# Attention scores from pairs of 64-row matmuls, in a trunk layer with three branches

## The chip, the core and the metric

The kernel runs on one core of one Trainium2 chip. The metric is the device time in microseconds (us) of one execution. The engines are named as in the profile: PE is TensorE with its matmuls, PEld are the loads of weights into it, DVE is VectorE, ACT is ScalarE, POOL is GpSimd, SP issues the DMAs.

## What is computed

Two layers of a hybrid trunk work on 1152 tokens (128 of context, 1024 latent), 1024 channels wide. Each layer projects the normalised stream once and feeds three branches: A is windowed attention with 8 heads of 64 channels, each latent block of 128 tokens seeing its neighbours and the cached context; B is a gated linear recurrence; C is differential attention with 4 heads of two softmax maps each, over all tokens. The branches are gated, projected, merged and projected again into the residual. What this case touches are the scores of A and C:

```
def diff_attn(q, k, v, lam, subln, lam_init):
    ...
    def block(qblk):
        s = jnp.einsum('bqhmd,bshmd->bhmqs', qblk, k).astype(jnp.float32) * SCALE
        p = jax.nn.softmax(s, axis=-1)
        pd = p[:, :, 0] - lam * p[:, :, 1]
        return jnp.einsum('bhqs,bshe->bqhe', pd.astype(v.dtype), v)
...
# branch A, one block of 128 queries, its window of keys (the cached context: the same with k_ctx)
s_w = jnp.einsum('bqkgd,bskd->bkgqs', qblk, kblk).astype(jnp.float32) * SCALE
```

All is float32. The dimension summed over in a score is 64, half of the 128 rows of PE.

## The kernel before, in words

Every value that goes into a product is split into a part rounded to fp32r, the format in which the products are taken (hi), and the rest (lo). A projection is then three products: hi by hi, hi by lo, lo by hi (`mm3`, L161 to L163, called for every large product). PE takes its instructions strictly in the program's order; that order is fixed when the program is built, by a planner that follows priorities and its own estimate of times. The attention has the higher priority, and the projections of the next head, the gates and the inputs of the recurrence run between its instructions ("background").

A layer begins with the unit phase (`unit_phase`): the four heads of branch C, one after the other, then branch A in four pairs of heads. For each group of one or two query tiles, `q_conv` transposes the queries (L440), `c_probs` or `a_probs` multiplies them with the keys (L538 and L539, L660 and L661) and computes the softmax, and `c_pv` or `a_pv` transposes the probabilities (L567, L700) and multiplies them with the values. In the profiled execution these phases lie at about 100 to 900 us (first layer) and 1500 to 2300 us (second). Behind each comes the tail with merge, branch products and recurrence, and then the output projection. The modulation stands at the very start: `mod_rows` multiplies with weights of 2 columns (L281) and transposes rows that have 2 partitions (L288).

For a score the 64 channels of hi and of lo of a key block are stacked to 128 rows, and the queries are copied into both halves of the rows before they are transposed (`qdup`), once as hi and once as lo. So a score is two matmuls over 128 rows, and these hold all four products:

```
T.matmul(out=p, lhsT=qh, rhs=kk, start=True, stop=False)
T.matmul(out=p, lhsT=ql, rhs=kk, start=False, stop=True)
```

PSUM has 8 banks of 512 float32 columns. Before, four are a ring for scores and projections (`ps("s")`), three for transposes (`"t"`), one for the sums with values (`"o"`).

Of the kernel before, what the change touches and what calls it, by code (L numbers as in the profile page):

```python
# [14 lines left out]
ALU = mybir.AluOpType  # L15
# [9 lines left out]
# priority offsets: attention of the units, branch products, modulation (beside the tail, w_out; its sums), recurrence  # L25
# [32 lines left out]
# rows of the per-layer table of short vectors  # L58
# [4 lines left out]
def hybrid_dit_kernel(ctx, tc, I, O):  # L63
# [5 lines left out]
    # buffers of each kind in PSUM  # L69
    PSB = {"s": 4, "t": 3, "o": 1}  # L70
# [51 lines left out]
    def rsqrt(x, n, scale, eps=None):  # L122
        """1/sqrt(x*scale + eps) of a [128, n] AP, n <= 12"""
# [15 lines left out]
    def split(hi, lo, raw, eh="A", el="P"):  # L139
        """hi = raw rounded to fp32r, lo = raw - hi"""  # L140
# [6 lines left out]
    def ws_load(wcols, kt):  # L147
        """[kt*128, 128] weight columns -> hi, lo [128, kt, 128]"""
# [29 lines left out]
    def ws_gemm(L, wcols, consume):  # L178
        """[128 cols, tokens] = W^T h^T, per chunk of 384 tokens"""
# [5 lines left out]
    def layer_vectors(l):  # L185
        """generator: loads the rows, two per step, then turns them into columns"""
# [25 lines left out]
    def layer_scalars(D):  # L212
# [12 lines left out]
        # lamc[3] = -(e1 - e2 + lam_init)  # L225
# [11 lines left out]
        # 4*softplus(-lam) = 4*(max(-lam, 0) + log1p(exp(-|lam|)))  # L237
# [21 lines left out]
    def silu_c():  # L259
        """[128, k, s]: silu of the two conditions, latent and context, in columns"""  # L260
# [13 lines left out]
    def mod_rows(D, b0, n):  # L274
        """blocks b0 to b0 + n by TensorE: the conditions' rows, then turned into columns; a step per load"""
# [156 lines left out]
    def q_conv(src, nb):  # L432
# [6 lines left out]
        for b in range(nb):  # L439
            T.transpose(p[:, b, :], e[:, b, :, :].rearrange("p s d -> p (s d)"), ident)  # L440
# [817 lines left out]
```

## Time and profile before

| | before |
|---|---|
| runs, us | 2894.25, 2898.65, 2900.79 |
| median, us | 2898.65 |
| span of the profiled execution, us | 2896.5 |
| PE busy | 2741.7 us, 95% |
| loads of weights (PEld) busy | 2651.9 us, 92% |
| DVE busy | 1753.5 us, 61% |
| ACT busy | 1272.5 us, 44% |
| POOL busy | 908.3 us, 31% |

The span runs from the first to the last instruction of the execution that was profiled; a run's time is taken around the whole execution. The share of PE counts a matmul from its start to the end of its way through the array, and the next one starts before that end; so the shares say which engine is in use, and the starts of following instructions say what one costs.

### The profile page before, as it was taken

How to read it: one execution, taken by the hardware profiler on the slowest of the kernel's cores; microseconds unless marked ns; L12 is line 12 of the kernel's file. 1: busy time of each engine (PE TensorE's matmuls, PEld its weight loads, DVE VectorE, ACT ScalarE, POOL GpSimd, SP SyncE). 2: the span in 40 equal slices, each digit the busy share in tenths (PEclk: the TensorE clock that was granted, in tenths of full speed). 3: DMA queues.
4: the chain of work that ended last, by engine and by line, in shares of the span. 5: the costliest groups of instructions: out<-in, count | busy, mean ns of one | idle time of the engine just before them, and what ended most of it. 6: DMA issues, size and time to landing. Idle time of an engine off the chain costs nothing.

```text
span 2896.5 us, 44162 instructions
## 1 busy us (share of the span) xinstructions
PE 2741.7 (95%) x16745; PEld 2651.9 (92%) x16745; DVE 1753.5 (61%) x4388; ACT 1272.5 (44%) x2569; POOL 908.3 (31%) x700
## 2 busy tenths in 40 slices
PE   8999999999997989998999999999999989899999
PEld 4989999999997989998999899998999979899989
DVE  5797878776536455116967887787665455311162
ACT  4464555566654531212144645555666446212110
POOL 1243344531234342213103343445212333322230
PEclk9999999999999999999999999999999999999999
DMA  6011011012221133114630110110112222311122
GB/s 227 25 33 32 21 32 42 31 52 73 67 75 62 58 128 108 49 41 140 191 107 25 33 34 19 33 48 31 55 63 80 66 66 64 110 41 52 48 89 85
DMA packets 231697, 190.74 MB, mean 66 GB/s; under 512 B 21746, under 2 KB 217660, under 8 KB 231484
## 3 DMA queue, kind: packets, MB, share of 16 engines
q1 hardware_dynamic: 231484, 187.92, 20.5%
q8 instruction: 132, 2.16, 0.3%
q14 instruction: 81, 0.66, 0.1%
HBM read 153.52 MB, written 34.35 MB: 65 GB/s over the span
## 4 chain that ended last, share of the span: by engine, by line
PE 47%; DVE 9%; ACT 3%; issue 2%; DMA 2%; POOL 1%; SPq 0%; DVEq 0%; POOLq 0%; ACTq 0%
PE ps_s L161 13%; PE ps_s L162 13%; PE ps_s L163 13%; DVE macc L110 2%; PE ps_o L709 1%; DVE lr L110 1%; PE ps_t L700 1%; DMA modw<-in_mod_w_dram 1%; DVE P L540 1%; PE ps_t L567 1%; PE ps_s L538 1%; PE ps_s L539 1%; DVE lu L110 1%; POOL li L101 0%; PE ps_s L660 0%
## 5 line engine op out<-in xcount | busy, mean ns | idle before, releaser
L161 PE MATMUL ps_s<-h,wsh 128*128 128x384 f32 x1920 | 661.1, 344 | 52.4 <-DVE yr L110 46.3
L163 PE MATMUL ps_s<-h,wsl 128*128 128x384 f32 x1920 | 655.3, 342 | 0.9 <-POOL wsl L101 0.9
L162 PE MATMUL ps_s<-h,wsh 128*128 128x384 f32 x1920 | 655.2, 341 | 0.0
L161 PEld LDWEIGHTS ps_s<-h,wsh 128*128 128x128 f32 x1920 | 364.7, 190 | 59.1 <-DVE yr L110 48.3
L163 PEld LDWEIGHTS ps_s<-h,wsl 128*128 128x128 f32 x1920 | 363.8, 190 | 2.0 <-POOL wsl L101 1.6
L162 PEld LDWEIGHTS ps_s<-h,wsh 128*128 128x128 f32 x1920 | 364.5, 190 | 0.6
L101 POOL TENSOR_TENSOR wsl<-wsraw,wsh 128x1024 fp32r<-128x1024 f32 x80 | 198.6, 2482 | 386.9 <-ACT wsh L98 184.1
L161 PE MATMUL ps_s<-uwh,h 128*128 128x384 f32 x864 | 297.6, 347 | 4.7 <-ACT h L98 2.1
L162 PE MATMUL ps_s<-uwl,h 128*128 128x384 f32 x864 | 294.9, 343 | 0.1
L163 PE MATMUL ps_s<-uwh,h 128*128 128x384 f32 x864 | 292.9, 345 | 0.0
L110 DVE SCALAR_TENSOR_TENSOR ps_s<-mg,ps_s 128x384 f32<-128x384 f32 x96 | 52.9, 559 | 353.2 <-PE ps_s L163 353.2
L101 POOL TENSOR_TENSOR qkraw<-qkraw,tab 128x384 f32<-128x384 f32 (+2 forms) x92 | 132.0, 1446 | 342.7 <-DVE qkraw L101 228.6
L540 DVE TENSOR_SCALAR_CACHE_REDUCE P<-ps_s 128x384 f32<-128x384 f32 (+1 forms) x400 | 205.5, 539 | 41.0 <-PE ps_s L539 40.0
L101 DVE TENSOR_TENSOR PT<-ps_t,PT 128x512 fp32r<-128x512 f32 (+2 forms) x304 | 187.6, 625 | 59.2 <-ACT PT L98 57.4
L161 PE MATMUL ps_s<-oh,wb 128*128 128x384 f32 x576 | 194.1, 347 | 26.3 <-DVE yr L101 9.4
L98 ACT ACTIVATE PT<-ps_t 128x512 fp32r<-128x512 f32 (+2 forms) x304 | 159.7, 546 | 124.3 <-PE ps_o L163 66.5
L550 ACT ACTIVATE P<-P,csm 128x1152 f32<-128x1152 f32 (+1 forms) x144 | 165.8, 1155 | 97.9 <-DVE csm L105 97.9
L957 ACT ACTIVATE mg<-ps_s 128x384 f32<-128x384 f32 x144 | 69.8, 486 | 307.2 <-PE ps_s L163 176.6
L162 PE MATMUL ps_s<-ol,wb 128*128 128x384 f32 x576 | 194.5, 344 | 0.0
L163 PE MATMUL ps_s<-oh,wb 128*128 128x384 f32 x576 | 194.3, 344 | 0.0
L161 PE MATMUL ps_s<-woh,yh 128*128 128x256 f32 x576 | 166.5, 290 | 11.8 <-DVE xt L101 6.5
L161 PEld LDWEIGHTS ps_s<-uwh,h 128*128 128x128 f32 x864 | 165.0, 191 | 8.5 <-DVE P L540 3.0
(252 smaller groups left out, 6320.8 us busy)
## 6 DMA issues: line engine op xcount, KB each, us to landing
wsraw<-in_w_in_dram SPq DMA_DIRECT2D x80, 512.0 KB, 3.7
wuraw<-in_w_in_dram SPq DMA_DIRECT2D x72, 192.0 KB, 3.5
ol<-osp SPq DMA_DIRECT2D x24, 576.0 KB, 3.8
modw<-in_mod_w_dram SPq DMA_DIRECT2D x16, 512.0 KB, 6.0
woraw<-in_w_out_dram SPq DMA_DIRECT2D x16, 512.0 KB, 4.4
modw<-in_mod_w_dram SPq DMA_DIRECT2D x14, 576.0 KB, 5.5
modw<-in_mod_w_dram SPq DMA_DIRECT2D x19, 384.0 KB, 4.1
wuraw<-in_w_in_dram SPq DMA_DIRECT2D x36, 128.0 KB, 2.3
```

What stands on the lines that cost most here:

```text
L98: A.activation(out=out, in_=in_, func=AF.Copy, scale=scale)
L101: e.tensor_tensor(out=out, in0=a, in1=b, op=op)
L110: V.scalar_tensor_tensor(out=out, in0=a, scalar=s, in1=b, op0=op0, op1=op1)
L161: T.matmul(out=out, lhsT=r(lh), rhs=r(rh), start=first, stop=False)
L162: T.matmul(out=out, lhsT=r(lh), rhs=r(rl), start=False, stop=False)
L163: T.matmul(out=out, lhsT=r(ll), rhs=r(rh), start=False, stop=last)
L538: T.matmul(out=p, lhsT=qh, rhs=kk, start=True, stop=False)
L539: T.matmul(out=p, lhsT=ql, rhs=kk, start=False, stop=True)
L540: V.tensor_scalar(out=S[:, n * c:n * c + n], in0=p, scalar1=1.0, scalar2=NEG, op0=ALU.mult, op1=ALU.max, accum_out=mx[:, mp, c:c + 1])
L550: A.activation(out=Ss[mp][:, 0:n], in_=Ss[mp][:, 0:n], func=AF.Exp, scale=0.125, bias=nm[:, mp:mp + 1], accum_out=acc)
L567: T.transpose(p[:, b, j * 128:(j + 1) * 128], Pm[:, (b0 + b) * 128:(b0 + b + 1) * 128], ident)
L957: A.activation(out=m, in_=p, func=AF.Tanh, scale=0.5)
```

## The change

The halves of the rows now hold two different things, and a score is taken over 64 rows. In branch C these are the two maps of a head, in branch A two heads. `q_conv` transposes a pair as it comes, without copies. `put_k` keeps hi and lo of the keys in buffers of their own. `qk_pair` issues three products for each of the two halves, alternating, and each half writes its own bank of a buffer of two banks. Lo by lo is no longer computed. In branch A the keys of a group are written into both halves, and the last two windows take their keys from two places, each with its own products.

PSUM is laid out anew: two banks for projections and the sums with values, two for transposes, and two buffers of two banks for scores, which branch products and every other output tile also use in the later phases.

```
-    PSB = {"s": 4, "t": 3, "o": 1}
+    PSB = {"s": 2, "t": 2, "q": 2}
...
-    def q_conv(src, nb):
-        e = al("E", "qdup", nb, 2, 64)
-        V.tensor_copy(e[:, :, 0, :], src)
-        acopy(e[:, :, 1, :], src)
-        q = al("Q", "qhl", 2, nb, 128)
-        p = ps("t", nb, 128)
-        for b in range(nb):
-            T.transpose(p[:, b, :], e[:, b, :, :].rearrange("p s d -> p (s d)"), ident)
+    def q_conv(src, nt):
+        q = al("E", "qhl", 2, nt, 128)
+        p = ps("t", nt, 128)
+        for b in range(nt):
+            T.transpose(p[:, b, :], src[:, b, :, :].rearrange("p s d -> p (s d)"), ident)
         acopy(r(q[:, 0]), p)
         tt(V, r(q[:, 1]), p, q[:, 0], ALU.subtract)
...
+    HALF = (slice(0, 64), slice(64, 128))
+    def qk_pair(pp, q, t, kh, kl):
+        for n, (qi, k) in enumerate(((0, kh), (0, kl), (1, kh))):
+            for hf, out in zip(HALF, pp):
+                T.matmul(out=out, lhsT=r(q[hf, qi, t, :]), rhs=r(k[hf]), start=n == 0, stop=n == 2)
...
     def c_probs(L, u, i, q, t):
-            for c in range(3 if i else 1):
-                n = 384 if i else 128
-                kk = r(u.k[mp][:, 3 * c:3 * c + 3, :] if i else u.xk[mp])
-                p = ps("s", n)
-                T.matmul(out=p, lhsT=qh, rhs=kk, start=True, stop=False)
-                T.matmul(out=p, lhsT=ql, rhs=kk, start=False, stop=True)
+        for c in range(3 if i else 1):
+            n = 384 if i else 128
+            kh, kl = (u.k[0][:, 3 * c:3 * c + 3, :], u.k[1][:, 3 * c:3 * c + 3, :]) if i else u.xk
+            pq = ps("q", 2, 512)
+            pp = [pq[:, mp, 0:n] for mp in range(2)]
+            qk_pair(pp, q, t, kh, kl)
...
-        po = ps("o", w)
+        po = ps("s", w)
```

What the planner makes of it stands in the order of PE's instructions. First a place in the first layer, head 0 of branch C, where scores are threaded into a projection. In a row, the line and the operation are followed by the output, the operands (names as in the program: `ck` keys, `qhl` queries, `uwh` and `uwl` or `wsh` and `wsl` weights, `h` the stream, `P` probabilities, `PT` their transposes, `uv` values) and the size of the output. Before:

```order
L162 MATMUL ps_s<-uwl,h 128x384
L538 MATMUL ps_s<-ck,qhl 128x384
L539 MATMUL ps_s<-ck,qhl 128x384
L538 MATMUL ps_s<-ck,qhl 128x384
L539 MATMUL ps_s<-ck,qhl 128x384
L163 MATMUL ps_s<-uwh,h 128x384
L161 MATMUL ps_s<-uwh,h 128x384
L162 MATMUL ps_s<-uwl,h 128x384
L163 MATMUL ps_s<-uwh,h 128x384
L161 MATMUL ps_s<-uwh,h 128x384
L538 MATMUL ps_s<-ck,qhl 128x384
```

A little later in the same head, of the changed program (L444 is the matmul in `qk_pair`, L562 the transpose in `c_pv`):

```order
L163 MATMUL ps_s<-h,wsl 128x384
L161 MATMUL ps_s<-h,wsh 128x384
L444 MATMUL ps_q<-ck,qhl 128x384 x6
L162 MATMUL ps_s<-h,wsh 128x384
L163 MATMUL ps_s<-h,wsl 128x384
L161 MATMUL ps_s<-h,wsh 128x384
L444 MATMUL ps_q<-ck,qhl 128x384 x6
L162 MATMUL ps_s<-h,wsh 128x384
L163 MATMUL ps_s<-h,wsl 128x384
L444 MATMUL ps_q<-ck,qhl 128x384 x6
L562 MATMUL ps_t<-ident,P 128x128 x6
```

Two matmuls for one map's chunk of scores have become six for the chunk of both maps, and between such runs stand three or two matmuls of a projection. The second place is where scores meet the products with values, again in head 0 of the first layer. Before:

```order
L161 MATMUL ps_o<-PT,uv 128x256
L538 MATMUL ps_s<-ck,qhl 128x384 x3
L567 MATMUL ps_t<-ident,P 128x128 x4
L162 MATMUL ps_o<-PT,uv 128x256
L163 MATMUL ps_o<-PT,uv 128x256
```

And of the changed program:

```order
L162 MATMUL ps_s<-PT,uv 128x256
L163 MATMUL ps_s<-PT,uv 128x256
L444 MATMUL ps_q<-ck,qhl 128x384 x2
L161 MATMUL ps_s<-PT,uv 128x256
L162 MATMUL ps_s<-PT,uv 128x256
L444 MATMUL ps_q<-ck,qhl 128x384 x4
L163 MATMUL ps_s<-PT,uv 128x256
L444 MATMUL ps_q<-ck,qhl 128x384
L161 MATMUL ps_s<-PT,uv 128x256
L444 MATMUL ps_q<-ck,qhl 128x384
L162 MATMUL ps_s<-PT,uv 128x256
```

The six of a chunk are now cut into shorter runs, down to a single matmul of 64 rows between two of 128. Counted over the whole program, the 1728 matmuls of 64 rows stand in 332 runs: 96 of them are one matmul long, 81 are six long, the longest are 36. Of the runs, 152 are followed by a transpose and 180 by another matmul. Before, 928 score matmuls stood among the others; 288 transposes of queries are now 144, and 100 of keys are 104.

## Rows read from the trace of the kernel before

**Rows 1.** The page's first part: span; busy us (share of span) and instructions.

```profile
span 2896.5 us, 44162 instructions
...
PE 2741.7 (95%) x16745; PEld 2651.9 (92%) x16745; DVE 1753.5 (61%) x4388; ACT 1272.5 (44%) x2569; POOL 908.3 (31%) x700
```

**Rows 2.** Windows of attention: length; busy us of PE, PEld, DVE, ACT, POOL; PEclk; DMA.

```profile
100.00:600.00 500.00, 479.90 (x3009) 461.88 (x3010) 403.34 (x1237) 267.61 (x564) 216.12 (x220) 0.98 0.10 30
600.00:900.00 300.00, 288.75 (x1750) 281.86 (x1749) 168.25 (x393) 170.57 (x372) 76.77 (x48) 0.98 0.21 68
1500.00:2000.00 500.00, 477.50 (x2994) 459.45 (x2994) 407.64 (x1271) 263.00 (x559) 193.85 (x200) 0.98 0.11 33
2000.00:2300.00 300.00, 298.42 (x1848) 290.32 (x1847) 179.54 (x460) 184.97 (x417) 87.30 (x63) 1.00 0.20 65
```

**Rows 3.** PE's waits, 100 to 900 us: first and last of 18 rows.

```profile
PE ps_s L161 <- DVE yr L110: 8.8, 1, 8.8
...
PE ps_s L161 <- DVE P L540: 0.2, 1, 0.2
```

**Rows 4.** Timeline of PE at 137 us: start, length, line, operation.

```profile
137.64 0.34 PE L162 MATMUL ps_s<-uwl,h 128*128 128x384 f32 x1
137.82 0.33 PE L538 MATMUL ps_s<-ck,qhl 128*128 128x384 f32 x1
137.99 0.33 PE L539 MATMUL ps_s<-ck,qhl 128*128 128x384 f32 x1
138.16 0.33 PE L538 MATMUL ps_s<-ck,qhl 128*128 128x384 f32 x1
138.33 0.34 PE L539 MATMUL ps_s<-ck,qhl 128*128 128x384 f32 x1
138.50 0.34 PE L163 MATMUL ps_s<-uwh,h 128*128 128x384 f32 x1
```

**Rows 5.** Timelines of PE at 621, 319, 313 and 227 us; rows of several merged.

```profile
621.44 0.39 PE L661 MATMUL ps_s<-ak,qhl 128*128 128x512 f32 x1
621.67 0.34 PE L161 MATMUL ps_s<-h,wsh 128*128 128x384 f32 x1
...
319.14 0.28 PE L161 MATMUL ps_o<-PT,uv 128*128 128x256 f32 x1
319.26 0.28 PE L162 MATMUL ps_o<-PT,uv 128*128 128x256 f32 x1
...
313.32 1.03 PE L567 MATMUL ps_t<-ident,P 128*128 128x128 f32 x8
...
227.36 1.05 PE L583 MATMUL ps_t<-one,sq 128*128 128x1 f32 x8
```

**Rows 6.** Loads of weights by line and shape: count | busy us, mean ns | idle before.

```profile
L161 PEld LDWEIGHTS ps_s<-h,wsh 128*128 128x128 f32 x1920 | 364.7, 190 | 59.1 <-DVE yr L110 48.3 <-ACT mg L957 4.7 <-DVE asm L666 3.5
...
L567 PEld LDWEIGHTS ps_t<-ident,P 128*128 128x128 f32 x584 | 68.7, 140 | 17.5 <-DVE P L110 9.1 <-DVE PT L101 3.8 <-PE ps_t L440 1.9
...
L281 PEld LDWEIGHTS ps_s<-modw,sc 128*2 128x2 f32 x64 | 5.6, 92 | 30.2 <-issue 27.2 <-DMA modw<-in_mod_w_dram 2.9
...
L288 PEld LDWEIGHTS ps_t<-ident,mrow 2*128 2x128 f32 x16 | 1.3, 136 | 4.5 <-ACT mrow L98 2.8 <-issue 0.9 <-ACT xsq L1142 0.9
```

**Rows 7.** Timelines of ACT at 38 us, of PE and PEld at 42 us.

```profile
37.73 0.59 ACT L98 ACTIVATE mrow<-ps_s 2x512 f32<-2x512 f32 x1 [9.02 <-PE ps_s L281]
...
40.54 2.31 PE L281 MATMUL ps_s<-modw,sc 128*2 128x512 f32 x5
...
41.83 1.02 PE L281 MATMUL ps_s<-modw,sc 128*2 128x512 f32 x2
42.78 0.41 PE L288 MATMUL ps_t<-ident,mrow 2*128 2x2 f32 x4
...
42.78 0.32 PEld L288 LDWEIGHTS ps_t<-ident,mrow 2*128 2x128 f32 x4 [0.86 <-issue]
43.11 0.09 PEld L281 LDWEIGHTS ps_s<-modw,sc 128*2 128x2 f32 x2
```

More of the change, by code (lines that the diff above doesn't have):

```diff
@@ L482, in qkv_gemm, with k_conv @@
             yield
-    def k_conv(u, cache, kdst):
+    def k_conv(u, cache, runs, put):
         kc = al("E", "kc", 128)
         dma(kc, cache)
-        kt = lambda i: u.kr[:, i, :, :].rearrange("p h d -> p (h d)")
-        for c in range(3):
-            p = ps("t", 3, 128)
-            for t in range(3):
-                b = 3 * c + t
-                T.transpose(p[:, t, :], kt(b + 1) if b < 8 else kc, ident)
-            for d0, d1, s, n in kdst(3 * c, 3):
-                put_k(d0, d1, p[:, s:s + n, :])
-        p = ps("t", 128)
-        T.transpose(p, kt(0), ident)
-        u.x = al("cx", "xkv", 4, 128)
-        u.xk = [u.x[:, 0], u.x[:, 1]]
-        put_k(u.xk[0], u.xk[1], p)
+        for n, blocks in enumerate(runs):
+            p = ps("t", len(blocks), 128)
+            for t, b in enumerate(blocks):
+                T.transpose(p[:, t, :], kc if b == 8 else u.kr[:, (b + 1) % 10, :, :].rearrange("p h d -> p (h d)"), ident)
+            put(n, p)
     def v_conv(u, cache, pair=False):
-        u.xv = [u.x[:, 2], u.x[:, 3]]
         u.v = [al("S", "uv", 9, 128) for _ in range(2)]
@@ L519, in c_kconv, with put @@
         u.k = [al("S", "ck", 9, 128) for _ in range(2)]
+        x = al("cx", "xkv", 5, 128)
+        u.xk, u.xv = (x[:, 0], x[:, 1]), (x[:, 2], x[:, 3])
+        def put(n, p):
+            hi, lo = [k[:, 3 * n:3 * n + 3, :] for k in u.k] if n < 3 else [k[:, None, :] for k in u.xk]
+            put_k(hi, lo, p)
         k_conv(u, I["cache_c_k"][0, L.l, :, h, :, :].rearrange("t m d -> t (m d)"),
-               lambda b0, n: [(u.k[0][:, b0:b0 + n, :], u.k[1][:, b0:b0 + n, :], 0, n)])
+               ((0, 1, 2), (3, 4, 5), (6, 7, 8), (9,)), put)
     def c_probs(L, u, i, q, t):
@@ L648, in a_probs @@
         for t, i in enumerate(tiles):
-            nb, m0 = 1, None
-            if i:
-                row, k0, nb, m0 = WIN[i - 1]
+            win, m0 = WIN[i - 1] if i else (None, None)
+            nb = sum(w[2] for w in win) if i else 1
             n = nb * 128
             S2 = al("P", "PA", 2, 512)
-            for j in range(2):
+            pq = ps("q", 2, 512)
+            pp = [pq[:, j, 0:n] for j in range(2)]
+            o = 0
+            for row, k0, m in win or ((0, 0, 1),):
+                kh, kl = [x[:, k0:k0 + m, :] for x in u.k[kv][row]] if i else u.xk[kv]
+                qk_pair([p[:, o:o + 128 * m] for p in pp], q, t, kh, kl)
+                o += 128 * m
+            for j, p in enumerate(pp):
                 b = 2 * t + j
@@ L657, in a_probs @@
                 Ps.append(S)
-                p = ps("s", n)
-                kk = r(u.k[kv][row][:, k0:k0 + nb, :] if i else u.xk[kv])
-                T.matmul(out=p, lhsT=r(q[:, 0, b, :]), rhs=kk, start=True, stop=False)
-                T.matmul(out=p, lhsT=r(q[:, 1, b, :]), rhs=kk, start=False, stop=True)
                 if m0 is None:
@@ L692, in a_pv @@
             else:
-                row, k0, nb, m0 = WIN[i - 1]
-                vs = [u.v[kv][:, b, :] for b in KROW[row][k0:k0 + nb]]
+                vs = [u.v[kv][:, b, :] for row, k0, m in WIN[i - 1][0] for b in KROW[row][k0:k0 + m]]
             for b0 in range(0, len(vs), 2):
@@ L813, in unit_phase @@
                 i, m = tiles[0], len(tiles)
[L814 removed]
+                q = fg(q_conv, (u.qs[g] if g else u.q)[:, i:i + m, :, :], m)
                 Ps = fg(a_probs, L, g, tiles, q)
@@ L1073, in w_out_phase @@
                 dma(x, x_in(l, i)[:, cs])
-                p = ps("s", 256)
+                p = ps("q", 2, 512)[:, 0, 0:256] if i % 2 else ps("s", 256)
                 ii = slice(i * 128, (i + 1) * 128)
```

68 lines of the change are left out of this document (30 added, 38 removed).

## Prediction

> **What bounds the kernel now.** I read the page's first lines first: TensorE (PE) has work in 2741.7 of 2896.5 us, the vector engine (DVE) in 1753.5 [rows 1]. The median of the runs, 2898.65 us, is 2.2 us above this span, so I make the sum against 2896.5 and add 2 us at the end. Then the stages, since the change touches only the attention of the two layers. It lies in four stretches of the view by windows [rows 2]: PE is busy 479.9 of 500, 288.8 of 300, 477.5 of 500 and 298.4 of 300 us there, at a granted clock of 0.98 to 1.00; DVE 403 of 500 and 168 of 300. So PE sets the end of these 1600 us, and the list of waits says how little else does: in the first layer's 800 us, PE's waits for others come to 33 us in 18 rows, from 8.8 us (which already belongs to the stage behind) down to 0.2 [rows 3]. A microsecond added to PE's own queue in attention comes out at the end nearly whole, and a microsecond taken off also.
>
> Busy time is no price, since a matmul's row lasts 0.33 us while the next starts sooner. I take starts from the timeline. Scores and projections follow each other every 0.17 to 0.18 us at 384 columns, and nothing opens between L162 and L538 [rows 4]; I use 0.175. At 512 columns it is 0.23, at 256 0.12. Eight transposes of 128 columns take 1.03 us with the last lasting 0.27, so 0.11 each; eight matmuls of one column, where only the load of 128 columns of weights can matter, take 1.05 with the last lasting 0.25, so 0.11 each too [rows 5]. That is the price of a load when nothing hides it behind a longer stream.
>
> **The scores themselves.** Before: 768 matmuls of 384 columns and 64 more in branch A at 0.175, 192 of 512 at 0.23, 64 of 128 at 0.11: 134 + 11 + 44 + 7 = 197 us. After, by the order of the changed program, 1728 matmuls of 64 rows: 1200 of 384 columns, 240 of 512, 144 of 256, 144 of 128, in pairs, one for each half of the rows. No row of this kernel has two such halves at work at once, so I bound their cost from both sides. From below, both matmuls of a pair, loads and streams, take the time of one: 600 x 0.175 + 120 x 0.23 + 72 x 0.12 + 72 x 0.11 = 149 us. From above, nothing overlaps: twice the streams, 298 us. In between, the two streams run side by side but the loads of weights go in one after another. A load here does not get cheaper with fewer rows: the transposes that load 2 rows (L288) take 136 ns, those of 128 rows 140 [rows 6]. Then the load is the limit, 0.11 us for each of the 1728 matmuls (0.23 for a pair of 512 columns, the same), 190 us. I take this middle value as the likeliest: in all of today's rows the next load goes beside the running stream, and none shows two loads at once. So three products instead of four bring 7 us, not the quarter that counting products would give.
>
> **Transposes.** Queries are no longer copied into both halves, so 144 of the 288 transposes fall away; the keys take 4 more. 140 x 0.11 = 15 us less. The copies on DVE and ScalarE that fed them go too; neither engine is the bound, so this can return only as part of PE's 33 us of waits in each layer.
>
> **Going between whole and half rows.** This is the term that decides. The kernel before has one place where PE turns to weights that use only a part of the array and back: the modulation at the start. L281 loads 2 columns of 128 rows, L288 loads 2 rows. The L281 matmuls start every 0.43 us (the fourth of five at 41.83, the first at 40.54), so the fifth at 42.26, and the next instruction should start at 42.69. It starts at 42.78, 0.09 late, and its load begins only then, with an idle of 0.86 us before it put down to nothing ("issue") [rows 7]; what it waits for, the row that ScalarE copies (mrow), was done at 38.32. On the way back the last of four loads, which take 0.32 us together with 0.136 for the last, began at 42.96, and the next load at 43.11: 0.15 instead of 0.06 later, 0.09 late again [rows 6, 7]. So, as I read it, such a turn empties the pipeline, and the load behind it is no longer hidden. The part of a load that is paid then is the difference between 128 columns and 2: 190 less 92 ns, 0.10 us, or for a transpose 140 less 92, 0.05 [rows 6].
>
> [...]
>
> How often? The program's order answers: the 64-row matmuls stand in 332 runs, as the pieces quoted with the change show, because scores are threaded between the projections and the products with values; 96 of the runs are a single matmul. Each run is entered (0.09 + 0.10) and left, 180 times toward a matmul (0.19) and 152 times toward a transpose (0.09 + 0.05): 63 + 34 + 21 = 119 us. And the last matmul of a run has to stream to its end, 0.175 us where I counted 0.11: 332 x 0.065 = 22 us.
>
> **PSUM.** Four banks for everything and one for the sums with values become two, with the scores' four apart; transposes have two where they had three. What could be late is a projection's chunk while the values' sum holds one of the two banks. The nearest price is PE's present waits, 33 us in a layer's attention [rows 3]: at best they shrink to nothing, at worst they double. With less work on DVE and a slower PE they should shrink; I take 10 us off over both layers. In the last stage the branch products move to the scores' banks, and four banks serve as before: nothing.
>
> **Sum.** -7 - 15 + 119 + 22 - 10 = +109 us; 2896.5 + 109 + 2 gives 3007 us, 3.7% slower.
>
> **The rivals.**
> *Loads side by side.* If two halves load at once as well, a pair costs what one costs: 149 instead of 197 us, and no tail of 22: -48 - 15 + 119 - 10 = +46, 2944 us. For it: the halves share no rows. Against it: nothing in the trace shows two loads at once. [...]
> *No overlap at all.* The halves take turns: 298 instead of 197, -15, +119, -10: +195, 3093 us. For it: every pair of rows today is one stream behind the other. Against it: the two halves have their own rows and their own banks.
> *No price for the turn.* If 64 rows of 128 columns behave as the whole array, nothing is drained and loads stay hidden; then -7 - 15 (and no tail) = -22, 2877 us, or with loads side by side -63, 2836 us. This one ends on the other side. For it: the two observed turns involve 2 columns or 2 rows. Against it: the same 0.09 us at both. It decides from the price of a turn: with 664 turns the change is faster only if one costs under 0.03 us with loads in turn, or under 0.095 with loads side by side.
>
> **How the numbers follow.** Loads in turn with turns paid 0.47; loads side by side, paid, 0.18; no overlap, paid, 0.13; no price 0.20, of which something near 0.12 at 2877; the rest is small. The likeliest case alone spans about 2970 to 3045 us: the price of a turn is known to a hundredth or two (664 x 0.02 = 13 us), and PSUM to 30. The range of 2925 to 3095 us takes in the first two cases whole and most of the third, about 8 in 10. Under 0.2% (6 us) a measurement of this kernel can't tell a difference; the only way there is a turn of nearly the deciding price, 0.03. Faster 0.20, slower 0.77.
>
> **What would show it.** Starts of 64-row matmuls 0.11 us apart within a run (0.09 or less: loads side by side; 0.175: no overlap). Before and behind each run an idle of PE put down to issue, the load beginning late. The transposes of queries counted 144. Attention stretches longer by some 50 us a layer, the stage behind them as long as before. The prediction is wrong if the rows inside runs are dense and the rows around them also: then the turn is free; or if PE in attention starts to wait for ScalarE or DVE by far more than 33 us a layer: then the banks are the cause.

## The result, and the profile after

The changed kernel takes 3142.7 us (median of four runs, 3142.35 to 3150.07) against 2899.4 of the kernel before (2894.25 to 2900.79). The ratio is 1.085, with a 95% interval of 1.084 to 1.087: 243 us more. The prediction had the direction (slower), but its 3007 us were 136 short and its range ended at 3095.

The page's first part answers to [rows 1]:

```profile
span 3140.6 us, 44957 instructions
...
PE 2869.9 (91%) x17245; PEld 2639.2 (84%) x17245; DVE 1736.9 (55%) x4276; ACT 1230.2 (39%) x2457; POOL 896.7 (29%) x700
```

PE was busy 95% of the span and is now 91%: the span grew by 244 us, PE's busy time by 128. The same four windows as in [rows 2]:

```profile
100.00:600.00 500.00, 448.87 (x2753) 389.66 (x2751) 340.97 (x1006) 210.99 (x427) 170.30 (x177) 0.93 0.09 28
600.00:900.00 300.00, 281.34 (x1733) 251.72 (x1732) 177.81 (x508) 161.52 (x385) 83.93 (x72) 0.98 0.16 51
1500.00:2000.00 500.00, 445.83 (x2886) 398.68 (x2885) 346.81 (x1005) 186.93 (x425) 122.00 (x122) 0.94 0.19 59
2000.00:2300.00 300.00, 268.90 (x1657) 238.89 (x1655) 201.19 (x587) 140.12 (x307) 114.67 (x118) 0.94 0.11 33
```

In 500 us of the first layer PE was busy 480 us before, at a granted clock of 0.98; now 449, at 0.93. For the first the prediction's sum had only the -10 us of PSUM, for the second no term. PE's waits (48 to 915 us; total, times, longest), which answer to [rows 3], first six of 26:

```profile
PE ps_t L492 <- DVE ak L101: 11.0, 3, 7.1
PE ps_s L162 <- DVE PT L101: 8.0, 8, 2.2
PE ps_q L444 <- DVE P L535: 7.4, 10, 1.9
PE ps_q L444 <- ACT qhl L98: 6.9, 6, 2.2
PE ps_s L161 <- ACT PT L98: 5.7, 4, 2.0
PE ps_s L161 <- ACT h L98: 4.9, 5, 1.8
```

All 26 rows come to 76 us, those of the second layer to 86; over the same stages they were 25 and 23 before. No row is large: PE waits a little everywhere, for the two engines that empty PSUM, at times for a bank (L444 for DVE's reading of earlier scores), at times for an operand that they make (L162 for PT).

Inside the runs of half rows the timeline of PE shows this, at 166 us (answers to [rows 4]):

```profile
165.91 0.33 PE L161 MATMUL ps_s<-h,wsh 128*128 128x384 f32 x1
166.18 0.79 PE L444 MATMUL ps_q<-ck,qhl 64*128 64x384 f32 x6
166.90 0.44 PE L162 MATMUL ps_s<-h,wsh 128*128 128x384 f32 x1
167.18 0.34 PE L163 MATMUL ps_s<-h,wsl 128*128 128x384 f32 x1
```

Six matmuls of 64 rows take 0.72 us from their first start to the start of the next instruction. Three streams of 0.175 are 0.525, so the two halves run side by side. The loads do as well (PEld at 146 us):

```profile
146.41 0.47 PEld L444 LDWEIGHTS ps_q<-ck,qhl 64*128 64x128 f32 x6 [0.64 <-DVE P L535]
```

Six loads within 0.47 us, and each lasts 0.18 to 0.19: in the trace the two loads of a pair start 3 ns apart (146.412 and 146.415), and so do its two matmuls (146.414 and 146.417). That was the prediction's second case, loads side by side, and not the one it took.

Around the runs the price of the turn is there as worked out. From 165.91 to 166.18 are 0.27 us instead of 0.175; the run takes 0.72 instead of 0.525; the first matmul behind it 0.28 instead of 0.175. That is 0.095 + 0.195 + 0.105 = 0.39 us for a run with two borders, 0.2 each, as the prediction had it (0.09, by its reading of the rows for emptying the pipeline, and 0.10 for a load that is no longer hidden).

**Where the 243 us are.** I sort the distances between the starts of successive matmuls, from the first projection of the first layer to the last matmul of the kernel. After a matmul of 384 columns up to 0.175 us is *stream* (0.232 for 512, 0.118 for 256, 0.11 for a transpose, nothing to the partner of a pair that starts with it). What is more, up to one stream and only where the granted clock was 0.50, is *half clock*. At a change between half and whole rows up to 0.21 us, and behind the first matmul after it up to 0.13, are *border* (0.4 and 0.26 at half clock). Of the remainder, distances over 0.3 us are *waits*, the others *rest*. The caps are choices, so a term is good to some 10 us. The kernel before ran again beside every experiment, at 2894 to 2900 us; ratios and differences of an experiment to it are against those runs. For all kernels of this study (us; the last column is the median of the runs):

| kernel | stream | borders (number) | half clock | waits | rest | median |
|---|---|---|---|---|---|---|
| before | 2560 | 0 | 43 | 156 | 85 | 2899 |
| after | 2515 | 109 (664) | 85 | 278 | 101 | 3143 |
| new_banks | 2565 | 0 | 110 | 361 | 125 | 3215 |
| pairs_old_banks | 2579 | 152 (894) | 55 | 128 | 75 | 3044 |
| whole_rows | 2502 | 0 | 113 | 362 | 94 | 3130 |
| six_whole | 2641 | 0 | 61 | 248 | 94 | 3105 |
| whole_old_banks | 2497 | 0 | 58 | 174 | 85 | 2866 |
| one_half | 2562 | 184 (896) | 73 | 126 | 62 | 3062 |
| new_banks_one_half | 2567 | 218 (1008) | 170 | 279 | 84 | 3370 |
| pob_atomic | 2511 | 141 (478) | 197 | 402 | 110 | 3415 |
| before_t2 | 2559 | 0 | 47 | 234 | 93 | 2995 |
| before_sums_in_s | 2561 | 0 | 66 | 184 | 81 | 2945 |
| before_own_scores | 2559 | 0 | 73 | 265 | 100 | 3047 |
| own_sums | 2560 | 0 | 105 | 312 | 100 | 3136 |
| singles | 2564 | 0 | 107 | 360 | 98 | 3183 |
| after_own_sums | 2518 | 115 (688) | 153 | 430 | 102 | 3357 |
| half_transposes | 2546 | 0 | 63 | 198 | 95 | 2957 |
| half_transposes_pool | 2544 | 0 | 58 | 212 | 90 | 2960 |

After against before: -45 stream, +109 borders, +42 half clock, +122 waits, +16 rest. The two terms that the prediction put at -10 and at nothing, waits and clock, are more than the borders. The added waits lie in the two unit phases: 59 us before and 182 after (48 and 162 by the rows of waits above), with 97 and 96 outside them. This sorts PE's time; it doesn't say what taking one term away would give back. The experiments ask that.

### The profile page after: what moved, and what is told of

Same layout as the page of the kernel before. It is cut to its first block, busy times and chain, and to the rows that moved or that the text cites. A ratio compares the mean times of both kernels' runs of the same rounds, so it can differ in the third digit from the quotient of the medians.

```text
span 3140.6 us, 44957 instructions
## 1 busy us (share of the span) xinstructions
PE 2869.9 (91%) x17245; PEld 2639.2 (84%) x17245; DVE 1736.9 (55%) x4276; ACT 1230.2 (39%) x2457; POOL 896.7 (29%) x700
## 5 line engine op out<-in xcount | busy, mean ns | idle before, releaser
L161 PE MATMUL ps_s<-h,wsh 128*128 128x384 f32 x1920 | 670.6, 350 | 32.7 <-ACT mg L953 23.2
L162 PE MATMUL ps_s<-h,wsh 128*128 128x384 f32 x1920 | 662.2, 345 | 0.0
L161 PEld LDWEIGHTS ps_s<-h,wsh 128*128 128x128 f32 x1920 | 369.2, 192 | 46.7 <-ACT mg L953 25.4
L162 PEld LDWEIGHTS ps_s<-h,wsh 128*128 128x128 f32 x1920 | 369.1, 192 | 3.7 <-issue 3.5
L161 PE MATMUL ps_s<-uwh,h 128*128 128x384 f32 x864 | 309.1, 359 | 18.6 <-ACT h L98 6.9
L162 PE MATMUL ps_s<-uwl,h 128*128 128x384 f32 x864 | 303.3, 351 | 4.5 <-POOL uwl L101 4.3
L163 PE MATMUL ps_s<-uwh,h 128*128 128x384 f32 x864 | 301.2, 352 | 0.0
L110 DVE SCALAR_TENSOR_TENSOR ps_q<-mg,ps_q 128x384 f32<-128x384 f32 x96 | 53.8, 560 | 357.9 <-PE ps_q L163 356.8
L535 DVE TENSOR_SCALAR_CACHE_REDUCE P<-ps_q 128x384 f32<-128x384 f32 (+1 forms) x400 | 199.1, 540 | 72.9 <-PE ps_q L444 72.6
L161 PE MATMUL ps_q<-oh,wb 128*128 128x384 f32 x576 | 196.4, 349 | 24.0 <-DVE yr L101 19.5
L101 POOL TENSOR_TENSOR qkraw<-qkraw,tab 128x384 f32<-128x384 f32 (+2 forms) x92 | 118.6, 1300 | 311.7 <-DVE qkraw L101 218.0
L162 PE MATMUL ps_q<-ol,wb 128*128 128x384 f32 x576 | 201.1, 349 | 4.2 <-POOL ol L101 4.2
L444 PE MATMUL ps_q<-ck,qhl 64*128 64x384 f32 x1152 | 175.8, 383 | 27.8 <-ACT qhl L98 14.6
L163 PE MATMUL ps_q<-oh,wb 128*128 128x384 f32 x576 | 199.8, 348 | 0.0
L101 POOL TENSOR_TENSOR uwl<-wuraw,uwh 128x1152 fp32r<-128x1152 f32 (+1 forms) x36 | 89.0, 2472 | 308.9 <-ACT uwh L98 260.7
```

Source lines behind the costliest of these rows:

```text
L101: e.tensor_tensor(out=out, in0=a, in1=b, op=op)
L110: V.scalar_tensor_tensor(out=out, in0=a, scalar=s, in1=b, op0=op0, op1=op1)
L161: T.matmul(out=out, lhsT=r(lh), rhs=r(rh), start=first, stop=False)
L162: T.matmul(out=out, lhsT=r(lh), rhs=r(rl), start=False, stop=False)
L163: T.matmul(out=out, lhsT=r(ll), rhs=r(rh), start=False, stop=last)
L444: T.matmul(out=out, lhsT=r(q[hf, qi, t, :]), rhs=r(k[hf]), start=n == 0, stop=n == 2)
```

## The experiments

**1. The layout alone: new_banks.** The kernel before with the new banks; both maps of a chunk in one buffer (so the loop over chunks goes around that over maps), scores over whole rows as before.

```
-    PSB = {"s": 4, "t": 3, "o": 1}
+    PSB = {"s": 2, "t": 2, "q": 2}
...
+            pq = ps("q", 2, 512)
...
-                p = ps("s", n)
+                p = pq[:, mp, 0:n]
...
-        po = ps("o", w)
+        po = ps("s", w)
```

> The kernel before with nothing but the changed kernel's layout of PSUM: two banks for projections and sums with values, two for transposes, two buffers of two banks for scores; a score is still two matmuls over 128 rows, and both maps of a chunk fill the two banks of one buffer. No matmul of 64 rows, no turn. Theory 'turns' (runs of 64-row matmuls cost PE about 0.19 us at each border, and nothing else matters): 2890 to 2915 us, PE waits in attention near the 25 us a layer of before. Theory 'banks' (the new layout lets PE wait for the engines that empty PSUM, 76 and 86 us a layer in the changed kernel instead of 25 and 23, and the clock falls behind such waits): 2990 to 3080 us, with PE waits in attention of over 60 us a layer.

3215.2 us, ratio 1.109 (1.107 to 1.111): 317 us, more than the whole change, and beyond what either theory said. Waits +205, half clock +67. The layout costs, without a pair in it. Its waits in the second layer's unit phase, first four of the list:

```profile
PE ps_q L539 <- DVE P L541: 18.2, 24, 2.2
PE ps_s L711 <- ACT PT L98: 11.7, 9, 2.8
PE ps_t L568 <- DVE P L110: 11.7, 13, 1.3
PE ps_s L161 <- ACT PT L98: 8.4, 9, 1.5
```

Outputs in all three rings appear, but only the first row is a wait for a bank, that of scores which DVE has still to read. The others wait for an operand: the transposes for P from DVE, the products with values for PT, as the groups of the same stage show:

```profile
L161 PE MATMUL ps_s<-PT,uv 128*128 128x256 f32 x144 | 44.2, 307 | 8.5 <-ACT PT L98 8.4
L711 PE MATMUL ps_s<-PT,uv 128*128 128x256 f32 x226 | 42.7, 302 | 19.2 <-ACT PT L98 11.7 <-DVE PT L101 6.5 <-DVE gate L110 0.7
```

As I read it, PE's order is planned so that something else stands where a bank or an operand is not yet ready; where the planned cover is too short, the wait shows up at whatever comes next. So the rows tell that PE waits, not which ring is to blame; experiments 6 to 10 ask that.

**2. The pairs alone: pairs_old_banks.** The changed kernel, each half in its own bank of the old ring of four.

```
-    PSB = {"s": 2, "t": 2, "q": 2}
+    PSB = {"s": 4, "t": 3, "o": 1}
...
-            pq = ps("q", 2, 512)
-            pp = [pq[:, mp, 0:n] for mp in range(2)]
+            pp = [ps("s", n) for _ in range(2)]
```

> The changed kernel with the PSUM layout of before (four banks for scores and projections, three for transposes, one for sums with values); each half of a pair has its own of the four banks. The scores stand in 447 runs here instead of 332, so there are 894 borders. Theory 'turns and banks': pairs side by side save 48 us, transposes 15, and 447 runs cost about 447 x 0.19 entering, 249 x 0.19 and 198 x 0.14 leaving = 160 us: about +97, 2980 to 3010 us, with attention's PE waits back at about 30 us a layer. Theory 'pairs alone' (all of the 243 us comes from the half rows, and banks have no part): 0.73 us for each of 332 runs gives at least 3140, and 3200 us or more with 447.

3044.4 us, 1.051 (1.049 to 1.052): 146 us more than before, 98 less than the change with its banks. PE's waits are below those of before (12 and 17 us a layer); the first two rows of the first layer:

```profile
PE ps_t L492 <- DVE ukr L101: 2.6, 1, 2.6
PE ps_s L444 <- DVE P L534: 2.4, 3, 1.8
```

The time is 34 us above the expected range, and the timeline shows where it goes, at 307 us:

```profile
307.08 0.39 PE L161 MATMUL ps_o<-PT,uv 128*128 128x256 f32 x1
307.40 0.79 PE L444 MATMUL ps_s<-ck,qhl 64*128 64x384 f32 x3
308.12 0.39 PE L162 MATMUL ps_o<-PT,uv 128*128 128x256 f32 x1
```

Three matmuls of one half take the 0.79 us that six of both halves took above. Where the second bank came later, the planner issued one half's three products alone; 806 of the 1728 streams have no partner beside them, and the stream term is 2579 instead of 2497 us. With a buffer of two banks this is rarer (112 streams in the changed kernel), but the buffers take banks from the rest of the kernel.

**3. and 4. No borders: whole_rows and whole_old_banks.** In the changed kernel, and in pairs_old_banks, three matmuls over all rows stand for the three pairs; they mix the scores of the two halves.

```
-        for n, (qi, k) in enumerate(((0, kh), (0, kl), (1, kh))):
-            for hf, out in zip(HALF, pp):
-                T.matmul(out=out, lhsT=r(q[hf, qi, t, :]), rhs=r(k[hf]), start=n == 0, stop=n == 2)
+        for out, qi, k, first, last in ((pp[0], 0, kh, True, False), (pp[0], 0, kl, False, True), (pp[1], 1, kh, True, True)):
+            T.matmul(out=out, lhsT=r(q[:, qi, t, :]), rhs=r(k), start=first, stop=last)
```

> The changed kernel with three matmuls over 128 rows in place of the six over 64 (two into the first bank, one into the second), which take PE's stream the same time as three pairs side by side; the scores of the two maps or heads are mixed by this, so that what is computed is not the reference's. Layout of PSUM, copies and transposes stay. No border between half and whole rows is left. Theory 'turns and banks': the 664 borders at 0.18 to 0.2 us go, 119 to 130 us, and the waits stay: 3010 to 3030 us. If the half clock of the changed kernel also came from the borders: 2940 to 2980. Theory that a border costs nothing (banks alone are the cause): 3130 to 3150 us.

> The pairs with the PSUM layout of before (pairs_old_banks, 3044 us), with three matmuls over 128 rows in place of six over 64: the scores of the two maps or heads are mixed, and no border between half and whole rows is left. In the changed layout the same edit gave back 13 us of 243. Theory 'hidden borders' (a border always takes PE about 0.19 us; in the changed layout PE had to wait for emptied banks anyway, so that time without borders became waits): here, where PE does not wait, the 894 borders give back 160 us or more: 2830 to 2880 us, below the kernel before by about the 63 us of side-by-side scores and fewer transposes. Theory 'borders cost little' (13 us is their whole price, and the form of the pairs is what is slow): 3020 to 3045 us.

whole_rows: 3129.8 us, 1.080 (1.078 to 1.081). Without any border the changed kernel is only 13 us faster; the waits are 84 us longer and the half clock costs 28 more. whole_old_banks: 2865.9 us, 0.990 (0.988 to 0.992), 178 us below pairs_old_banks: 152 of borders and 82 of streams without partners, less 46 of waits and 3 of half clock and 10 of rest. It is the only one here under the time of before. Its stream term is 63 us below; as three whole matmuls count like three pairs side by side, the 48 + 15 us that the prediction had for the scores and the transposes come out by construction. What the run shows is what is left of them at the end, 28 us, as the other terms eat more than half. So the idea would be worth about 1% if turns were free, every stream had a partner and banks were not short.

With these runs the two layouts stand beside each other three times, with nearly all else alike: new_banks is 317 us over before, the changed kernel 98 over pairs_old_banks, whole_rows 264 over whole_old_banks. The layout costs time each time. The planner makes a new order for each kernel, so what is shown is the layout together with the order planned for it.

**5. The border alone: one_half.** The kernel before, its PSUM and number of matmuls unchanged; the second product of a score over 64 rows.

```
-                T.matmul(out=p, lhsT=ql, rhs=kk, start=False, stop=True)
+                hf = slice(64 * mp, 64 * mp + 64)
+                T.matmul(out=p, lhsT=ql[hf], rhs=kk[hf], start=False, stop=True)
...
```

> The kernel before, where the second product of each score (lo of the queries by the keys) is taken over only the 64 rows that hold hi of the keys, so that lo by lo is left out; as many matmuls of as many columns as before, the same PSUM. 544 matmuls of 64 rows in 448 runs, 896 borders. Theory 'turns': 0.19 us entering and 0.14 to 0.19 leaving, 150 to 170 us: 3040 to 3070 us, with PE's waits for ScalarE and DVE no longer than before. If only the drain is paid and the load stays hidden, about 0.1 us a border: 2980 to 3000. If a border costs nothing: 2890 to 2910 us.

3062.0 us, 1.056 (1.054 to 1.058): +164 us, inside the range of theory 'turns'. Its timeline has the price bare, whole and half rows in turn:

```profile
143.29 0.44 PE L540 MATMUL ps_s<-ck,qhl 64*128 64x384 f32 x1
143.66 0.44 PE L538 MATMUL ps_s<-ck,qhl 128*128 128x384 f32 x1
144.03 0.44 PE L540 MATMUL ps_s<-ck,qhl 64*128 64x384 f32 x1
144.40 0.33 PE L161 MATMUL ps_o<-PT,xkv 128*128 128x128 f32 x1
```

```profile
143.66 0.19 PEld L538 LDWEIGHTS ps_s<-ck,qhl 128*128 128x128 f32 x1 [0.19 <-issue]
144.03 0.18 PEld L540 LDWEIGHTS ps_s<-ck,qhl 64*128 64x128 f32 x1 [0.19 <-issue]
```

Starts are 0.37 us apart instead of 0.175, and every load starts with its matmul, after an idle that nothing explains ("issue"), instead of beside the stream before. 0.195 us a border; 896 of them at that would be 175, and 184 were counted.

**6. to 10. Which banks.** Five divisions of the eight banks in the kernel before, scores over whole rows throughout (s projections, t transposes, o sums with values, c scores):

```
-    PSB = {"s": 4, "t": 3, "o": 1}
+    PSB = {"s": 5, "t": 2, "o": 1}            # before_t2
+    PSB = {"s": 5, "t": 3}                    # before_sums_in_s: ps("o", ..) -> ps("s", ..)
+    PSB = {"s": 2, "t": 3, "o": 1, "c": 2}    # before_own_scores: scores ps("c", n)
+    PSB = {"s": 2, "t": 2, "o": 1, "c": 3}    # own_sums
+    PSB = {"s": 2, "t": 2, "c": 4}            # singles: sums in s
```

> The kernel before with one of the three banks for transposes given to the ring of scores and projections (five, two and one). Which part of the new layout costs 317 us without any pair? Theory 'transposes' (two banks for transposes are too few, since a bank is held until ScalarE and DVE have copied it): most of it, 3050 us or more. Theory 'projections' (two banks for projections, of which the sums with values take one for long): 2895 to 2930 us here, since projections have more banks than before.

> The kernel before with the new layout, but the four banks of the scores each by itself instead of two buffers of two: two banks for projections and sums, two for transposes, four for scores; the branch products and the output stay with the two of the projections. new_banks, with the pairs of banks, took 3215 us. Theory 'pairs of banks' (a buffer of two is free only when both halves are emptied, so two buffers are too few): near 2900 to 2960 in attention's share, that is a unit phase of 770 to 800 us instead of 900. Theory 'projections': unit phases of 870 to 910 us as in new_banks. The stages behind can be longer than in new_banks by the narrower ring there.

> As singles (two banks for projections and sums, two for transposes, four single ones for scores; 3183 us, unit phases of 892 and 893 us), but one bank of the scores goes to the sums with values: projections two, transposes two, sums one, scores three. Theory 'sums' (a sum holds one of the two banks of the projections through all its blocks of keys, so that a projection can't begin while the one before is copied): the unit phases fall most of the way, to 780 to 830 us each, 2960 to 3060 us in all. Theory 'two banks for projections are too few in any case': 860 to 890 us, and 3120 to 3180 in all. If the scores were what wants banks, longer than in singles.

> The kernel before with its ring of four divided: two banks for projections, two for scores; three for transposes and one for sums as before. Against own_sums one bank more for transposes and one less for scores. Theory 'sums': with sums and transposes as before only the division is left, and that costs little: unit phases 765 to 790 us, 2900 to 2950 us. Theory 'two banks for projections are too few': unit phases of 830 us and more, over 3020 us.

> The kernel before, sums with values in the ring of scores and projections, which gets the bank of the sums: five and three banks. Theory 'sums': what hurts is a sum in a ring of two; in a ring of five four are left for the others, as before: 2890 to 2920 us. If sharing a ring is itself what hurts (the order in which its banks are given out): 2950 us or more.

2995, 3183, 3136, 3047 and 2945 us (ratios 1.034, 1.100, 1.082, 1.051, 1.016, each to within 0.003). No single theory came out. The two unit phases together, 1531 us before, are 1582 in before_t2, 1785 in singles, 1657 in own_sums, 1655 in before_own_scores and 1581 in before_sums_in_s; new_banks has 1804. From these: that buffers of two must be empty together costs little (new_banks over singles, 19, with the loops exchanged as well). A bank taken from the transposes and given to the common ring costs 51. Sums in the common ring, which has five then, cost 50, where I had expected nothing. Taking the scores out of the common ring, so that projections and scores have two banks each, costs 124 with all else as before. And putting the sums into the two of the projections costs 127 more (singles over own_sums, although singles has a bank more for scores). The last two are the greater part of the 273 us from before to new_banks. They stand in a row: 124 for the divided ring, 3 for a bank moved from transposes to scores (own_sums over before_own_scores), 127 for the sums, 19 for the pairs of banks. A third bank for transposes was worth 51 beside a common ring and about nothing here, so such prices don't carry from one division to another. Theory 'sums' was half right: they matter most where they sit in a ring of two.

**11. Longer runs: pob_atomic.** pairs_old_banks with the six matmuls of a chunk as one piece for the planner.

```
+        with tc.tile_critical():
+            for n, (qi, k) in enumerate(((0, kh), (0, kl), (1, kh))):
...
```

> The pairs with the PSUM layout of before, and the six matmuls of a chunk issued in one piece, with nothing between them: 239 runs of half rows instead of 447, the shortest six long. Theory 'price per border': 208 runs less at 0.36 us each, 75 us: 2955 to 2985 us. Theory 'price per half-row matmul' (their number, 1728, stays): 3030 to 3050 us. If the pieces hold banks longer and PE waits for DVE because of it, the gain is smaller, with PE's waits in attention above the 12 to 17 us a layer of pairs_old_banks.

3414.6 us, 1.180 (1.178 to 1.182), against both theories. The order has 239 runs as meant, and only 18 streams without partner. But PE's waits are 167 and 172 us a layer, and two of their rows name, by the profile, what a piece waited for:

```profile
PE ps_s L445 <- DVE csm L539: 11.6, 6, 2.6
PE ps_s L445 <- POOL ol L101: 7.9, 2, 4.0
```

A score reads neither `csm` (the maxima behind it) nor `ol`. The piece waits for more than its operands, and the run says nothing of the price of a border.

**12. Fewer transposes: half_transposes, half_transposes_pool.** The kernel before; a pair of query blocks is transposed as it comes, and both halves are filled behind the transposes, by ScalarE and DVE alone or with the second halves by GpSimd.

```
-        e = al("E", "qdup", nb, 2, 64)
-        V.tensor_copy(e[:, :, 0, :], src)
-        acopy(e[:, :, 1, :], src)
...
+        for b in range(nb // 2):
+            T.transpose(p[:, b, :], src[:, 2 * b:2 * b + 2, :].rearrange("p m d -> p (m d)"), ident)
...
+            for hf in (slice(0, 64), slice(64, 128)):
+                acopy(r(qt[hf, 0, :, mp, :]), p[s])
...
```

> The kernel before with the one part of the change that saves PE time without half rows or new banks: the query tiles are transposed a pair at a time, 144 transposes instead of 288, and the two halves are filled from PSUM by four copies of ScalarE and four subtractions of DVE over 64 rows, instead of two copies ahead of the transposes and two operations behind them. 144 transposes less at 0.11 us: 16 us, 2876 to 2888 us. The other theory: the eight short operations hold the bank of the transposes longer and the scores begin later; PE waits for them, 2895 to 2930 us.

> half_transposes (2957 us), in which a bank of the transposes is emptied by four operations of ScalarE and DVE over 64 rows, into half of the rows each, and the other halves are then filled by four copies of GpSimd. Theory 'DVE is late': the eight operations delay DVE's reading of scores (PE's wait for it is 21 us there), and with four less most of the 16 us of PE time comes through: 2875 to 2890 us. The other theory: the scores wait for GpSimd instead, 2900 to 2960 us.

2957.0 us (1.020, 1.018 to 1.022) and 2960.4 (1.022, 1.020 to 1.024). The 14 and 16 us of stream are saved, as priced, and 42 and 56 us of waits and 20 and 15 of half clock come in their place. With GpSimd the wait for DVE's reading of the scores falls from 21 to 8 us and others take its place. Why a longer way from the queries to the scores costs so much was not settled: other orders are planned in both.

**13. Borders in the new layout: new_banks_one_half, six_whole.** The first puts the edit of one_half into new_banks. The second is the changed kernel with each of the six matmuls over all rows, which mixes the scores of the two halves. Its edit:

```
             for hf, out in zip(HALF, pp):
-                T.matmul(out=out, lhsT=r(q[hf, qi, t, :]), rhs=r(k[hf]), start=n == 0, stop=n == 2)
+                T.matmul(out=out, lhsT=r(q[:, qi, t, :]), rhs=r(k), start=n == 0, stop=n == 2)
```

> new_banks (scores over whole rows in the new layout, 3215 us) with the edit of one_half: the second product of each score over only the 64 rows that hold hi of the keys, lo by lo left out. 544 matmuls of 64 rows and, each alone or nearly, up to 896 borders or more are added. In the layout of before the same edit cost 164 us. Theory 'hidden borders' (in the new layout PE waits for emptied banks anyway, and the time of a border only shortens such a wait): 3215 to 3270 us, with PE's waits in attention well below the 205 us of new_banks. Theory 'a border always adds its price': 3365 to 3390 us, waits as before.

> The changed kernel with all six matmuls of a chunk over 128 rows (the scores are mixed by this): no borders, and no two side by side, in nearly the order of the changed kernel (1719 of 16973 matmuls stand at another place; in whole_rows, with three, nearly all did). By the starts of following matmuls in the traces, the changed kernel's two unit phases have 1316 us of streams, 109 at borders, 182 of waits over 0.3 us and 54 of half clock; six streams instead of three pairs add about 131 us, and no border takes away 109. Theory 'order' (borders and waits stand side by side in the changed kernel; in whole_rows only another order made the waits longer): 22 us more, 3150 to 3175 us, waits of 160 to 190. Theory 'ScalarE and DVE set the time' (PE's time, borders or streams, fits into waits): waits fall by about as much as streams grow, and the time is 3060 to 3120 us, with waits under 120.

new_banks_one_half: 3369.8 us, 1.163 (1.160 to 1.165), 155 us over new_banks. 'Hidden borders' falls by its time, and only in part is anything hidden: of 218 us at borders only 82 disappear from the waits and 41 from the rest, and the half clock takes 60 back. six_whole: 3105.4 us, 1.073 (1.071 to 1.075). Six streams one after the other are 37 us faster than six in pairs: +126 of stream, -109 of borders, -24 half clock, -30 waits, -7 rest. Neither theory's numbers held whole; waits of 150 us in the unit phases lie between. Against whole_rows it has 139 us more stream and is yet 24 us faster, with 114 less waits and 52 less half clock. So here less work for PE did not come out at the end: with less of it PE waited longer. It is no rule of this layout, since in new_banks_one_half most of the added work did come out (155 of 218 us).

**14. Another division for the pairs: after_own_sums.** The changed kernel with one buffer of two banks for the scores, and a bank of their own for the sums.

```
-    PSB = {"s": 2, "t": 2, "q": 2}
+    PSB = {"s": 2, "t": 3, "o": 1, "q": 1}
...
```

> The changed kernel with another division of the eight banks: two for projections, three for transposes, one for the sums with values, and one buffer of two for the scores, in place of two, two and two buffers of two. Theory 'rings of projections and transposes' (scores need few banks; a sum in the ring of the projections and a third bank less for transposes are what costs): unit phases of 820 to 855 us instead of 864 and 876, fewer waits, 3050 to 3110 us. Theory 'scores': a single buffer of two can't be filled while it is emptied: 3150 us or more, with waits of scores for DVE's copies on top of the list.

3357.2 us, 1.160 (1.157 to 1.163), the second theory. First rows of the waits of the whole kernel:

```profile
PE ps_s L161 <- ACT mg L953: 79.7, 79, 5.1
PE ps_q L444 <- DVE P L535: 75.1, 54, 2.7
```

The scores wait for DVE to empty their only buffer (75 us, where the changed kernel has 13), and in the stages behind the projections for the merge wait for ScalarE to read them (80 us, there 23). So for pairs in buffers of two, one buffer is too few. Two are half of PSUM, and other ways to divide the other half than that of the change were not run.

## Why the prediction was wrong, step by step

- *What bounds the kernel* held for the kernel before: there PE's microseconds come out at the end (one_half: +164 for 184 at borders). It was then taken to hold for the kernel after, where 109 us of borders taken away gave back 13 (whole_rows).
- *The scores themselves*: the step "I take this middle value as the likeliest", loads one after another, failed. Pairs run side by side with their loads; -7 should have been near -48, and the tail of 22 does not exist. With the transposes that would be -63; the changed kernel has -45, since 112 streams find no partner (112 x 0.175 = 20). The bound from below was the right value, but for those. (The number of score matmuls before is 1088, as the sums have it; the 928 in the section on the change is a slip.)
- *Transposes*: -15 held as stream. half_transposes, which fills the halves by eight operations behind the transposes where the change has two, came out 57 us longer; what the shorter way costs in the changed kernel can't be told from the rest.
- *Turns*: 119 us predicted, 109 counted at the same 332 runs; the price (0.2 us with the load) came from two rows of a wholly different shape and held. That 64-row matmuls would pay it at both ends of a run was the author's estimate, which no row of before shows; the runs showed 109 us at 664 borders (0.16 each) in the changed kernel and 0.195 us a border in one_half, with loads that begin only with their matmul. That it is the pipeline that empties there is the author's reading and was not shown.
- *PSUM* is the step that failed by most: "at best they shrink to nothing, at worst they double ... I take 10 us off". The waits grew by 122 us, and the granted clock, for which the sum had no term, cost 42 more. PE's waits in a kernel with rings of four and three banks were no bound for rings of two; as I read it, they are what is left over after an order was planned round its banks. new_banks shows the cost of the layout without the pairs, +317, and pairs_old_banks the pairs without it, with waits of 12 and 17 us a layer instead of 76 and 86. Even the worst case named, a doubling, adds 33 us a layer, 66 over both, and the span of the likeliest case took 30. (The sums of the rival without a price for the turn, -22 and -63, leave the -10 out.) The prediction had named the sign, waits by far more than 33 us a layer, "then the banks are the cause"; it had given it no price.
- *Nothing in the last stage*: about right. The two stages behind are 18 and 17 us longer, of which 28 are streams: 154 more matmuls of projections and 12 of attention now come after the first branch product.
- By the prediction's own rival with loads side by side the sum was +46. With all terms as counted, -45 + 109 + 122 + 42 + 16 = +244. So the 136 us that the prediction was short are a difference: 190 too little for waits, clock and rest, 55 too much for scores, tail and turns. That the two partly cancel is luck. And the sign: no price for the turn would not have saved it here, as whole_rows shows (3130).

What stays open: why 109 us of borders taken away give back 13 in whole_rows. That its waits are longer is shown, and its order is another one in part: with the scores left out, 2590 of the other 15517 matmuls of PE stand at another place by operands and size (in six_whole 1101). The expectation of six_whole says nearly all; a count by place in the whole order comes out that way, since three matmuls for six shift the place of all that follow. six_whole keeps more of the order and changes the streams. How much is the order and how much the layout was not separated. A kernel with pairs that beats the one before was not found. whole_old_banks is 28 us below before, and a run costs about 0.39, so by this estimate it would need fewer than about 70 runs of half rows in the old banks, all with partners; there are 447.

## What to carry to other kernels

Bound a change of PSUM by running the layout alone, not by the waits of the present one: here waits of 33 us a layer stood beside 317 us for the layout. A run of half-row matmuls costs PE about 0.39 us at its two ends here, a little more than two streams of 384 columns (0.35), so by this estimate half rows can pay only in few and long runs; no kernel here shows that they do. And where a stage waits for other engines, work taken off PE can return as waits and as a lower granted clock, as in whole_rows (109 us less at borders, 84 more of waits and 28 more of half clock).

## What the runs showed of the chip

The granted clock also fell where no wait stands ahead. Windows of one_half (columns as in [rows 2]); from 141 to 148.2 us PE changes 17 times between whole and half rows:

```profile
141.00:148.20 7.20, 7.20 (x27) 4.04 (x25) 5.69 (x20) 1.79 (x6) 6.61 (x11) 1.00 0.00 0
148.20:151.60 3.40, 3.40 (x10) 3.07 (x11) 1.77 (x10) 2.60 (x5) 1.37 (x2) 0.50 0.01 2
151.60:156.00 4.40, 4.40 (x22) 3.59 (x22) 1.98 (x4) 3.96 (x7) 2.49 (x1) 1.00 0.32 92
```

By its busy share PE was never idle; yet the clock was granted at 0.50 for 3.4 us behind that stretch. The share hides the borders, since a matmul's row there lasts 0.44 us instead of 0.33: sorted as above, 3.8 of the 7.2 us are streams and 3.6 borders. Over the two unit phases one_half has 133 us at half clock where the kernel before has 41, with PE's waits at 26 instead of 48 us. That it is the borders, and not the half rows at work alone or something else, is not shown: pairs_old_banks has 894 borders and 85 us at half clock, whole_old_banks none and 85 too, with waits of 29 and 55 us. Behind a wait it looks like this, in the changed kernel:

```profile
168.50:171.80 3.30, 1.31 (x9) 0.67 (x9) 3.05 (x12) 2.91 (x6) 0.64 (x1) 0.99 0.00 0
171.80:178.60 6.80, 4.88 (x19) 4.04 (x20) 6.80 (x16) 1.20 (x2) 2.37 (x1) 0.50 0.22 61
```

In another such stretch, at 435 us (granted 0.50 from 434.6 to 444.8 us), matmuls that go one after the other cost 0.32 us instead of 0.175:

```profile
435.07 0.52 PE L161 MATMUL ps_s<-h,wsh 128*128 128x384 f32 x1
435.39 0.52 PE L162 MATMUL ps_s<-h,wsh 128*128 128x384 f32 x1
435.71 0.52 PE L163 MATMUL ps_s<-h,wsl 128*128 128x384 f32 x1
```

So where the clock fell behind a wait here, the wait was paid twice in part: once itself, and once in the streams behind it. In new_banks the half clock is 67 us more than before, beside 205 us more of waits.
